# Batch normalization over 64 tiles: each of the two DMA rings is given one transfer at a time

## The chip, the cores and the metric

The kernel runs on one core of a Trainium2 chip. The metric is the device time of one execution in microseconds (us). A TensorE clock of 1.0 is granted in the run, and TensorE does no work here.

## The reference

```python
def reference(x, gamma, beta, running_mean, running_var):   # x: 32 x 256 x 128 x 128 float32
    eps = 1e-5
    ...                                                     # the four vectors, one value per channel
    return gamma * (x - mean) / np.sqrt(var + eps) + beta
```

Every element of x is multiplied by one number of its channel and another number is added. x has 537 MB and so has the result: 1,074 MB pass between HBM and the on-chip memory.

## The kernel before

x is seen as 64 tiles of 128 partitions (128 channels) by 16384 float32, 8.39 MB each; a partition's row is 64 KB and contiguous in HBM. There are three tile buffers, `bufs[0]` to `bufs[2]`, and tile i lives in buffer i mod 3. The work on a tile is a load, one operation in place, and a store:

- SyncE (SP) issues all loads (line 94 for tiles 1 to 63). Its queue is one DMA ring, q1 in the profile. Tile 0 comes in two pieces (lines 84 and 91), with four small loads of the channel vectors between them (line 87).
- VectorE (DVE) scales and shifts the tile in place: `compute`, line 122, one instruction over 16384 columns. For tile 0 there are two, for the last tile VectorE does 9216 columns and ScalarE the other 7168 (line 145).
- ScalarE (ACT) issues all stores: `store`, line 133. Its queue is the other ring, q10.

Both rings are served by the same 16 DMA engines: each transfer is spread over all 16, eight rows of 64 KB to an engine, and each engine adds one to the transfer's semaphore when its own eight rows are through. A transfer has ended when its semaphore has risen by 16.

The order is kept by semaphores written out by hand. `loaded[s]` counts the loads into buffer s, `stored[s]` the stores from it, `done` the operations. A load of tile i waits until the store of tile i - 3 has ended, since both use one buffer; a store waits for its tile's operation. Nothing else holds a load or a store back. So a load can be issued while the load before it is still running, and a store while the store before it is running: the second one then queues on the ring behind the first.

Before the loop, a short chain on VectorE and ScalarE (lines 85 to 117) turns the four vectors into one scale and one shift for each channel; it ends before the first quarter of tile 0 is worked on.

Of the kernel before, what the change touches and what calls it, by code (L numbers as in the profile page):

```python
# [1 line left out]

# [4 lines left out]


NBUF = 3

VCOLS = 9216


@with_exitstack
def kernel(
    ctx: ExitStack,
    tc: tile.TileContext,
    x: bass.AP,
    gamma: bass.AP,
    beta: bass.AP,  # L20
    running_mean: bass.AP,
    running_var: bass.AP,
    out: bass.AP,
):
    nc = tc.nc
    eps = 1e-5
    f32 = mybir.dt.float32

    N, C, H, W = x.shape
    P = nc.NUM_PARTITIONS  # L30
    assert C % P == 0
    NCB = C // P
    HW = H * W
    NT = N * NCB
    B = 32
    NQ = P // B
    NE = 16
    NPAR = 4

    xr = x.rearrange("n (cb p) h w -> (n cb) p (h w)", p=P)  # L40
    outr = out.rearrange("n (cb p) h w -> (n cb) p (h w)", p=P)

    params = ctx.enter_context(tc.tile_pool(name="params", bufs=1))
    data = ctx.enter_context(tc.tile_pool(name="data", bufs=1))
    bufs = [data.tile([P, HW], f32, name=f"t{s}", tag=f"t{s}") for s in range(NBUF)]
    rows = params.tile([B, NPAR * C], f32, name="rows", tag="rows")
    turned = params.tile([B, NPAR * C], f32, name="turned", tag="turned")
    par = params.tile([P, NPAR, NCB], f32, name="par", tag="par")
    eps_t = params.tile([P, 1], f32, name="eps_t", tag="eps")
    std_t = params.tile([P, NCB], f32, name="std_t", tag="std")  # L50
    rstd_t = params.tile([P, NCB], f32, name="rstd_t", tag="rstd")
    scale_t = params.tile([P, NCB], f32, name="scale_t", tag="scale")
    ms_t = params.tile([P, NCB], f32, name="ms_t", tag="ms")
    shift_t = params.tile([P, NCB], f32, name="shift_t", tag="shift")

    loaded = [tc.alloc_semaphore(f"loaded{s}") for s in range(NBUF)]
    stored = [tc.alloc_semaphore(f"stored{s}") for s in range(NBUF)]
    early = tc.alloc_semaphore("early")  # L60
    done = tc.alloc_semaphore("done")
    fetched = tc.alloc_semaphore("fetched")
    vec = tc.alloc_semaphore("vec")
    act = tc.alloc_semaphore("act")

    with tc.tile_critical():  # L66
        count = [0]

        def step(inst, sem=None, value=None):

            if sem is not None:
                inst._wait_ge(sem, value)
            elif count[0]:
                inst._wait_ge(vec, count[0])
            inst.then_inc(vec, 1)
            count[0] += 1
            return count[0]

        left, right = slice(0, HW // 4), slice(HW // 4, HW)
        last = NT - 1  # L80

        nc.sync.dma_start(out=bufs[0][:, left], in_=xr[0][:, left]).then_inc(early, 16)
        zeroed = step(nc.vector.memset(rows[:], 0.0))  # L85
        for r, ap in enumerate((running_var, gamma, beta, running_mean)):
            inst = nc.sync.dma_start(out=rows[0:NE, r * C : (r + 1) * C], in_=ap.partition_broadcast(NE))  # L87
            if r == 0:
                inst._wait_ge(vec, zeroed)
            inst.then_inc(fetched, 16)  # L90
        nc.sync.dma_start(out=bufs[0][:, right], in_=xr[0][:, right]).then_inc(loaded[0], 16)  # L91
        for i in range(1, NT):
            s, turn = i % NBUF, i // NBUF
            inst = nc.sync.dma_start(out=bufs[s][:], in_=xr[i]).then_inc(loaded[s], 16)
            if turn:
                inst._wait_ge(stored[s], 16 * turn)


        step(nc.vector.memset(eps_t[:], eps))  # L99
        step(nc.vector.transpose(out=turned[:], in_=rows[:]), fetched, 16 * NPAR)  # L100

        blocks = turned.rearrange("p (rc q b) -> p rc q b", q=NQ, b=B)
        flat = par.rearrange("p r cb -> p (r cb)")
        for q in range(NQ):
            placed = step(nc.vector.tensor_copy(out=flat[q * B : (q + 1) * B], in_=blocks[:, :, q, 0]))  # L105
        var_t, gamma_t, beta_t, mean_t = (par[:, r] for r in range(NPAR))
        nc.scalar.activation(  # L107
            out=std_t[:],
            in_=var_t,
            func=mybir.ActivationFunctionType.Sqrt,  # L110
            bias=eps_t[:],
            scale=1.0,
        )._wait_ge(vec, placed).then_inc(act, 1)
        step(nc.vector.reciprocal(out=rstd_t[:], in_=std_t[:]), act, 1)  # L114
        step(nc.vector.tensor_mul(out=scale_t[:], in0=gamma_t, in1=rstd_t[:]))  # L115
        step(nc.vector.tensor_mul(out=ms_t[:], in0=mean_t, in1=scale_t[:]))  # L116
        ready = step(nc.vector.tensor_sub(out=shift_t[:], in0=beta_t, in1=ms_t[:]))  # L117
        nc.vector.wait_ge(vec, ready)

        def compute(i, cols=slice(0, HW)):  # L120
            t, cb = bufs[i % NBUF], i % NCB
            return nc.vector.tensor_scalar(  # L122
                out=t[:, cols],
                in0=t[:, cols],
                scalar1=scale_t[:, cb : cb + 1],
                scalar2=shift_t[:, cb : cb + 1],
                op0=mybir.AluOpType.mult,
                op1=mybir.AluOpType.add,
            ).then_inc(done, 1)

        def store(i, after):
            s = i % NBUF
            nc.scalar.dma_start(out=outr[i], in_=bufs[s][:])._wait_ge(done, after).then_inc(stored[s], 16)  # L133

        compute(0, left)._wait_ge(early, 16)
        compute(0, right)._wait_ge(loaded[0], 16)
        store(0, 2)
        for i in range(1, last):
            compute(i)._wait_ge(loaded[i % NBUF], 16 * (i // NBUF + 1))
            store(i, i + 2)  # L140

        turns = last // NBUF + 1
        compute(last, slice(0, VCOLS))._wait_ge(loaded[last % NBUF], 16 * turns)
        t, cb = bufs[last % NBUF], last % NCB
        nc.scalar.activation(  # L145
            out=t[:, VCOLS:],
            in_=t[:, VCOLS:],
            func=mybir.ActivationFunctionType.Identity,
            bias=shift_t[:, cb : cb + 1],
            scale=scale_t[:, cb : cb + 1],  # L150
        )._wait_ge(loaded[last % NBUF], 16 * turns).then_inc(done, 1)
        store(last, last + 3)

        for s in range(NBUF):
            nc.sync.wait_ge(stored[s], 16 * ((NT - s + NBUF - 1) // NBUF))


# [1 line left out]
_INS = ['x', 'gamma', 'beta', 'running_mean', 'running_var']  # L159
_OUTS = [((32, 256, 128, 128), 'float32')]  # L160


# [23 lines left out]
```

## Time and profile before

| what | value |
|---|---|
| median of the runs | 2505.82 us (2505.62 to 2506.52, 3 runs) |
| profiled execution, its own time | 2505.62 us |
| its span | 2503.8 us |
| DMA, mean over the span | 429 GB/s |
| share of the 16 engines' span, loads (q1) and stores (q10) | 49.8% and 49.6% |
| VectorE busy | 564.0 us (23%) |
| a load from issue to landing, median | 58.3 us |
| a store from issue to landing, median | 49.8 us |

The span is what the trace covers; the execution's own time is 1.8 us longer. The first lines of the profile's page say how long each engine was busy; the section on the DMA queues says what share of the time of all 16 DMA engines the packets of each ring took. "Issue to landing" counts from the instruction that starts a transfer to the last increment of its semaphore, so time spent queued on the ring is in it. The trace also holds a record of each DMA packet, with its ring, start, duration and size, and the time of each semaphore increment. A packet of this kernel's large transfers is one row of 64 KB.

### The profile page before, as it was taken

Reading aid. Unit: us, or ns where it says so; the run is one execution under the profiler, and the core shown is the slowest. Engines: PE = TensorE matmul, PEld = TensorE weight load, DVE = VectorE, ACT = ScalarE, POOL = GpSimd, SP = SyncE. Lnnn points to the kernel's source line nnn. Section 1 sums busy time; section 2 is a strip of 40 time slices with the busy share of each in tenths; the row PEclk is TensorE's granted clock in tenths of the full one; section 3 lists DMA queues with packets and bytes.
Section 4 is the critical chain, followed back from the end, with each engine's and each line's share of the span. In section 5 each row is a group of like instructions: output and inputs, shape, how many; then the busy total and the mean of one; then the engine's idle time right before and its main releaser. Section 6 shows DMA issues by size and latency. Waiting matters only on the chain.

```text
span 2503.8 us, 266 instructions
## 1 busy us (share of the span) xinstructions
DVE 564.0 (23%) x76; ACT 7.9 (0%) x3; POOL 0.2 (0%) x4
## 2 busy tenths in 40 slices
DVE  3121221212212122121221212212122122221220
ACT  0000000000000000000000000000000000000001
POOL 0000000000000000000000000000000000000000
DMA  9999999999999999999999999999999999999997
GB/s 419 434 436 431 428 430 433 434 434 433 432 436 432 433 433 427 430 429 433 436 431 429 428 432 433 429 428 436 432 429 428 434 434 429 426 434 435 436 434 316
DMA packets 18706, 1073.83 MB, mean 429 GB/s; under 512 B 2128, under 2 KB 2192, under 8 KB 2192
## 3 DMA queue, kind: packets, MB, share of 16 engines
q1 hardware_dynamic: 9488, 536.94, 49.8%
q10 hardware_dynamic: 9216, 536.88, 49.6%
q14 instruction: 2, 0.02, 0.0%
HBM read 536.94 MB, written 536.87 MB: 429 GB/s over the span
## 4 chain that ended last, share of the span: by engine, by line
another core or an unknown queue 75%; DVE 22%; DMA 2%; ACT 0%; issue 0%; SPq 0%; ACTq 0%; DVEq 0%
DVE t L122 22%; DMA t<-in_x_dram 2%; ACT t L145 0%; SPq L87 0%; DVE rows L85 0%; SPq L91 0%; ACTq L133 0%; DVE eps_t L99 0%; DVEq L181 0%; SPq L66 0%
## 5 line engine op out<-in xcount | busy, mean ns | idle before, releaser
L122 DVE TENSOR_SCALAR t<-t,scale_t,shift_t 128x16384 f32<-128x16384 f32 (+2 forms) x65 | 560.5, 8624 | 1903.6 <-DMA t<-in_x_dram 1903.4
L145 ACT ACTIVATE t<-t,shift_t,scale_t 128x7168 f32<-128x7168 f32 x1 | 6.4, 6361 | 2459.8 <-DMA t<-in_x_dram 2459.8
L100 DVE STREAM_TRANSPOSE turned<-rows 32x1024 f32<-32x1024 f32 x1 | 1.2, 1233 | 7.3 <-DMA rows<-in_running_mean_dram 7.3
L107 ACT ACT_TABLE_LOAD x1 | 1.3, 1283 | 0.9 <-SPq L66 0.9
L85 DVE MEMSET rows<- 32x1024 f32 x1 | 0.9, 912 | 1.2 <-SPq L66 1.2
L105 DVE COPY par<-turned 32x8 f32<-32x8 f32 x4 | 0.6, 162 | 0.1
L107 ACT ACTIVATE std_t<-par,eps_t 128x2 f32<-128x2 f32 x1 | 0.3, 295 | 9.4 <-DVE par L105 9.4
L114 DVE RECIPROCAL rstd_t<-std_t 128x2 f32<-128x2 f32 x1 | 0.2, 166 | 0.4 <-ACT std_t L107 0.4
L117 DVE TENSOR_TENSOR shift_t<-par,ms_t 128x2 f32<-128x2 f32 x1 | 0.2, 163 | 0.0
L116 DVE TENSOR_TENSOR ms_t<-par,scale_t 128x2 f32<-128x2 f32 x1 | 0.2, 161 | 0.0
L115 DVE TENSOR_TENSOR scale_t<-par,rstd_t 128x2 f32<-128x2 f32 x1 | 0.2, 161 | 0.0
L170 POOL MEMSET const-bfloat16-1.0<- 128x1 bf16 x1 | 0.1, 102 | 0.0
L170 POOL MEMSET const-uint8-127<- 128x1 uint8 x1 | 0.1, 102 | 0.0
L170 POOL MEMSET const-float32-0.0<- 128x1 f32 x1 | 0.1, 99 | 0.2 <-issue 0.2
L170 POOL MEMSET const-float32-1.0<- 128x1 f32 x1 | 0.1, 99 | 0.0
L99 DVE MEMSET eps_t<- 128x1 f32 x1 | 0.1, 59 | 0.1
## 6 DMA issues: line engine op xcount, KB each, us to landing
t<-in_x_dram SPq DMA_DIRECT2D x1, 6144.0 KB, 19.6
t<-in_x_dram SPq DMA_DIRECT2D x1, 2048.0 KB, 7.7
out_dram<-t ACTq DMA_DIRECT2D x64, 49.8
t<-in_x_dram SPq DMA_DIRECT2D x63, 58.3
rows<-in_running_var_dram SPq DMA_DIRECT2D x1, 16.0 KB, 6.4
rows<-in_gamma_dram SPq DMA_DIRECT2D x1, 16.0 KB, 6.2
rows<-in_beta_dram SPq DMA_DIRECT2D x1, 16.0 KB, 6.0
rows<-in_running_mean_dram SPq DMA_DIRECT2D x1, 16.0 KB, 6.1
```

Source lines behind the costliest of these rows:

```text
L85: zeroed = step(nc.vector.memset(rows[:], 0.0))
L99: step(nc.vector.memset(eps_t[:], eps))
L100: step(nc.vector.transpose(out=turned[:], in_=rows[:]), fetched, 16 * NPAR)
L105: placed = step(nc.vector.tensor_copy(out=flat[q * B : (q + 1) * B], in_=blocks[:, :, q, 0]))
L107: nc.scalar.activation(out=std_t[:], in_=var_t, func=mybir.ActivationFunctionType.Sqrt, bias=eps_t[:], scale=1.0,)._wait_ge(vec, placed).t ...
L114: step(nc.vector.reciprocal(out=rstd_t[:], in_=std_t[:]), act, 1)
L115: step(nc.vector.tensor_mul(out=scale_t[:], in0=gamma_t, in1=rstd_t[:]))
L116: step(nc.vector.tensor_mul(out=ms_t[:], in0=mean_t, in1=scale_t[:]))
L117: ready = step(nc.vector.tensor_sub(out=shift_t[:], in0=beta_t, in1=ms_t[:]))
L122: return nc.vector.tensor_scalar(out=t[:, cols], in0=t[:, cols], scalar1=scale_t[:, cb : cb + 1], scalar2=shift_t[:, cb : cb + 1], op0=myb ...
L145: nc.scalar.activation(out=t[:, VCOLS:], in_=t[:, VCOLS:], func=mybir.ActivationFunctionType.Identity, bias=shift_t[:, cb : cb + 1], scale ...
L170: nc = _bacc.Bacc("TRN2", target_bir_lowering=False, num_devices=1)
```

## The change

A load of tile i (for i from 2) now waits for the end of the load of tile i - 1 as well as for its buffer: the wait for the buffer becomes an instruction of its own on SyncE ahead of the load, and the load itself carries the wait for its predecessor. A store of tile i (for i from 1 to 62) is preceded on ScalarE by a wait for the end of the store of tile i - 1. The store of the last tile gets no such wait, and neither does the load of tile 1. Sizes, buffers, operations and the order of the instructions on each engine stay as they are; the line numbers after the first edit shift by 4.

```diff
         for i in range(1, NT):
             s, turn = i % NBUF, i // NBUF
+            if turn:
+                nc.sync.wait_ge(stored[s], 16 * turn)
             inst = nc.sync.dma_start(out=bufs[s][:], in_=xr[i]).then_inc(loaded[s], 16)
-            if turn:
-                inst._wait_ge(stored[s], 16 * turn)
+            if i >= 2:
+                inst._wait_ge(loaded[(i - 1) % NBUF], 16 * ((i - 1) // NBUF + 1))
...
         def store(i, after):
             s = i % NBUF
-            nc.scalar.dma_start(out=outr[i], in_=bufs[s][:])._wait_ge(done, after).then_inc(stored[s], 16)
+            inst = nc.scalar.dma_start(out=outr[i], in_=bufs[s][:]).then_inc(stored[s], 16)
+            inst._wait_ge(done, after)
+
+        def turn_of_store(i):
+            nc.scalar.wait_ge(stored[(i - 1) % NBUF], 16 * ((i - 1) // NBUF + 1))
...
         for i in range(1, last):
             compute(i)._wait_ge(loaded[i % NBUF], 16 * (i // NBUF + 1))
+            turn_of_store(i)
             store(i, i + 2)
```

## The prediction

> **What bounds the kernel now.** I read the page's first lines, then the DMA queues.
>
> ```profile
> span 2503.8 us, 266 instructions
> DVE 564.0 (23%) x76; ACT 7.9 (0%) x3; POOL 0.2 (0%) x4
> DMA  9999999999999999999999999999999999999997
> ...
> q1 hardware_dynamic: 9488, 536.94, 49.8%
> q10 hardware_dynamic: 9216, 536.88, 49.6%
> ```
>
> The two rings fill 99.4% of the time of the 16 DMA engines; no compute engine is near its limit. Then who waits for whom, of the engines and of SP's queue, and the issues with their time to landing:
>
> ```profile
> DVE t L122 <- DMA t<-in_x_dram: 1903.4, 64, 31.4
> ...
> SPq L94 <- DMA out_dram<-t: 2391.3, 61, 67.6
> ...
> out_dram<-t ACTq DMA_DIRECT2D x64, 49.8
> t<-in_x_dram SPq DMA_DIRECT2D x63, 58.3
> ```
>
> VectorE waits for loads and loads wait for buffers. 58.3 + 8.8 + 49.8 = 116.9 us is one turn of a buffer, three tiles, so a tile takes 39.0 us. Both transfers last longer than that: part of each is queueing behind its predecessor, and that queue is what the change removes.
>
> The period shows in the timeline, as the distance from one 128x16384 operation to the next (first column):
>
> ```profile
> 53.05 8.81 DVE L122 TENSOR_SCALAR t<-t,scale_t,shift_t 128x16384 f32<-128x16384 f32 x1 [22.79 <-DMA t<-in_x_dram]
> 93.26 8.81 DVE L122 TENSOR_SCALAR t<-t,scale_t,shift_t 128x16384 f32<-128x16384 f32 x1 [31.40 <-DMA t<-in_x_dram]
> ...
> 248.63 8.81 DVE L122 TENSOR_SCALAR t<-t,scale_t,shift_t 128x16384 f32<-128x16384 f32 x1 [29.88 <-DMA t<-in_x_dram]
> ...
> 406.19 8.81 DVE L122 TENSOR_SCALAR t<-t,scale_t,shift_t 128x16384 f32<-128x16384 f32 x1 [30.91 <-DMA t<-in_x_dram]
> 446.36 8.81 DVE L122 TENSOR_SCALAR t<-t,scale_t,shift_t 128x16384 f32<-128x16384 f32 x1 [31.36 <-DMA t<-in_x_dram]
> ...
> 2201.07 8.81 DVE L122 TENSOR_SCALAR t<-t,scale_t,shift_t 128x16384 f32<-128x16384 f32 x1 [29.86 <-DMA t<-in_x_dram]
> ...
> 2433.07 8.81 DVE L122 TENSOR_SCALAR t<-t,scale_t,shift_t 128x16384 f32<-128x16384 f32 x1 [29.83 <-DMA t<-in_x_dram]
> 2471.74 5.08 DVE L122 TENSOR_SCALAR t<-t,scale_t,shift_t 128x9216 f32<-128x9216 f32 x1 [29.85 <-DMA t<-in_x_dram]
> ```
>
> It is (2471.74 - 53.05) / 62 = 39.01 us on average, 38.84 in the four tiles from 93.26, 40.17 at its worst, and 38.67 in the six from 2201.07.
>
> The packet records say why. Per tile an engine moves 16 packets of 64 KB. The usual one takes 2.418 us, back to back, whether the rings alternate (from 35 us on) or one runs alone (loads at 23 to 32 us, the last store). That is 38.65 to 38.69 us per tile, the floor. The rest, 0.36 us per tile, is stretched packets (up to 1.5 us longer) on the engines furthest behind: following the records end to start, stretch comes to 12 us on the mean engine and about 22 us on the worst, over the run. The worst engines do not idle; the others wait for them. The 16 increments of a load's semaphore spread over 0.7 us at tile 1, 5 us around tile 9, 26 us from tile 32 to the end. So in the second half 11 or 12 engines have an empty ring whenever a load or store is issued: they already run with one transfer per ring. The other 4 or 5 never do. The change puts all 16 into that state and stops the drift.
>
> **The change, part by part.**
>
> *The gap in a ring.* Rows of the records: a contested ring gives its increment after the other ring's next packet, 2.4 + 0.3 us; the slowest engine adds at least 0.7 (tile 1's spread); SP issues 0.02 us after a landing (112.38 to 112.40); the first packet follows 0.9 us after issue on idle engines (last store), 2.6 us where engines are busy (the store at 1627). Sum 4.4 to 6.1 us, rounded up to whole packets: three, 7.3 us. In it the other ring runs alone at the same 2.418 us per packet, so the engine loses nothing while the two gaps do not meet. The fast engines of the second half show this: with gaps of about four packets in each ring, they follow at 38.67 us per tile. Cost: 0, covered by the other ring's transfer; if that cover is gone, see the third rival.
>
> The rule that speaks against the change is in the Trainium skill, "DMA: Bandwidth & Descriptors", section "Anatomy of one DMA — SWDGE (gpsimd) path": about 2.0 us fixed per transfer, mostly the receipt of the last byte. It is told for the other issue path; taken for all 124 transfers that now wait and laid bare, it would be an estimated 248 us more. The trace sides against laying it bare: a lone ring's packets fill the engine.
>
> *Do the gaps meet?* Count from the start. Load 1's last packets end at 49.5 to 50.3 us; store 0 began at 35.0, alternating, and has some five of its eight packets left. Load 1 lands at 53.0, load 2 starts at about 57; store 0 runs three packets alone, two alternating, ends at about 62 and lands near 65. Store 1 is issued then, 12 us after load 1 landed and 3 us after its operation ended (61.86). Each ring's gap now lies in the middle of the other's transfer, two packets or more off either end, and since both gaps are about the same length the lag should stay.
>
> *Starting a transfer on an empty ring.* This is what each load and store does now. The first store did so at 30.3 us with all engines in step: it stretched the packets in flight by 0.05 to 0.70 us, 0.46 on the mean. Over all stores that met an empty ring, the mean is 0.13 us per engine; for loads 0.01. So 0.14 us per tile, at most 0.46 + 0.01.
>
> *The stretch per tile afterwards.* What counts is the stretch of the engine that ends last. From below: the mean engine's whole-run stretch, 12/64 = 0.19 us. From above: the worst engine of each tile, added up as if every tile waited for it anew, 53.6 us over 63 tiles = 0.85. Between them: from 875 to 2125 us, where most engines start transfers on empty rings, the mean engine has 0.26 us per tile; the run's ratio of worst to mean, 22/12, makes that 0.47. I take 0.47, since rings with a gap still let an engine lag by a packet or two. Period 38.65 + 0.47 = 39.12, against 39.01: 62 x 0.11 = +7 us. Ends: 0.19 gives 62 x (38.84 - 39.01) = -10.5 us; 0.85 gives 62 x 0.49 = +30 us.
>
> *Queues and waits.* 61 wait instructions on SP and 62 on ACT lie inside the gaps. Behind SP's stands only the next load. Behind ACT's wait stand its store and, at the end, ScalarE's part of the last tile (L145): store 62 should be issued some 20 us before that tile lands, so it is in time; failing that, it costs up to its 6.4 us. The buffer wait is met long before the load's turn. Load 2, queued at 4.87 us before, is issued at 53.0; store 0 covers that.
>
> *The end.* Store 63 has no wait for its predecessor and joins the ring behind store 62, which has some packets left to cover the last operation (6.36 us), as now. Fast engines finish some 14 us early now and would not; that helps nobody. 0, at most 3 us.
>
> **Sum.** 2505.6 + 7 + 0 = 2512.6 us for the execution; the profiled run stands 0.2 us below the median, so 2512.6.
>
> **Rivals.**
> 1. *Staying in step is itself cheaper*: engines are stretched because they are out of step, so all tiles go like the early ones (38.84). For it: the stretch grew with the spread, to 39.3 and 40.17 at 3 to 8 us of it. Against: with the largest spread the period was lowest, 38.67. 2505.6 - 10.5 = 2495 us.
> 2. *Nothing changes*: the same engines carry the same stretch, 2505.6 us. For it: most engines already run so. Against: starts on empty rings become universal.
> 3. *Gaps meet*: stores are slower to restart than loads, the lag grows until load i and store i - 2 both wait for store i - 3. Both rings are then empty for 0.33 + 0.67 + 0.02 + 0.95 = 2.0 us per tile: 62 x 2.0 = +122 us, 2628. It decides once the lag grows from 12 to nearly a whole period of 39 us. Against: the fast engines show no such drift.
>
> **How the numbers follow.** A measurement of this kernel can tell about 0.2% (5 us) from no change. Forecast (2512.6, own range 2505 to 2532): 0.50, of which 0.10 ends within 5 us. Rival 1: 0.33, of which 0.30 is faster and 0.03 within. Rival 2: 0.10. Rival 3: 0.07. Faster 0.30, same 0.23, slower 0.47. The range 2492 to 2545 takes in the -10.5 end with a few us of scatter and the +30 end with the end's 3 and L145's 6; it leaves out rival 3 and tails of some 0.1.
>
> **What would show it.** Right: landings of a load spread under 5 us throughout; each ring with three or four packets' gap; DMA share still 99%; load issue to landing about 36 us and store about 34; a period near 39.1 without a late stretch at 38.67; SP waiting for loads, not stores. Rival 1: the period stays at 38.8. Rival 3: SP waits for stores, DMA share near 95%, period near 41. The prediction is wrong if an engine alone on one ring does not keep 2.418 us per packet, or if most starts cost the first store's 0.46 us (62 x 0.33 = +20 us on top).

## The result and the profile after

The changed kernel takes 2487.69 us (median of 4, 2485.97 to 2489.02) beside 2505.72 us, a ratio of 0.9928 with a 95% interval of 0.9911 to 0.9946: 0.7% faster, where I had said 0.3% slower. Its profiled execution takes 2486.43 us with a span of 2484.7. The page of the changed kernel:

```profile
span 2484.7 us, 389 instructions
DVE 564.0 (23%) x76; ACT 7.9 (0%) x3; POOL 0.2 (0%) x4
DMA  9999999999999999999999999999999999999999
...
q1 hardware_dynamic: 9488, 536.94, 50.1%
q10 hardware_dynamic: 9216, 536.88, 49.9%
```

The rings now fill the whole span, 100.0% against 99.4%. Then SP's queue waits and the issues:

```profile
SPq L98 <- DMA t<-in_x_dram: 1378.8, 62, 48.0
SPq L97 <- DMA out_dram<-t: 1009.0, 61, 16.8
...
out_dram<-t ACTq DMA_DIRECT2D x64, 38.6
t<-in_x_dram SPq DMA_DIRECT2D x63, 38.6
```

From load 2 to store 62 nothing queues on a ring any more: both transfers last one period. SP waits first for the buffer (line 97, the store of tile i - 3, at most 16.8 us) and then for the preceding load (line 98). The timeline:

```profile
52.87 8.81 DVE L126 TENSOR_SCALAR t<-t,scale_t,shift_t 128x16384 f32<-128x16384 f32 x1 [22.86 <-DMA t<-in_x_dram]
...
247.22 8.81 DVE L126 TENSOR_SCALAR t<-t,scale_t,shift_t 128x16384 f32<-128x16384 f32 x1 [29.91 <-DMA t<-in_x_dram]
...
401.81 8.81 DVE L126 TENSOR_SCALAR t<-t,scale_t,shift_t 128x16384 f32<-128x16384 f32 x1 [29.84 <-DMA t<-in_x_dram]
418.74 0.34 ACTq L137 DMA_DIRECT2D out_dram<-t  x1
440.43 8.81 DVE L126 TENSOR_SCALAR t<-t,scale_t,shift_t 128x16384 f32<-128x16384 f32 x1 [29.81 <-DMA t<-in_x_dram]
...
2415.80 8.81 DVE L126 TENSOR_SCALAR t<-t,scale_t,shift_t 128x16384 f32<-128x16384 f32 x1 [29.82 <-DMA t<-in_x_dram]
2454.43 5.08 DVE L126 TENSOR_SCALAR t<-t,scale_t,shift_t 128x9216 f32<-128x9216 f32 x1 [29.82 <-DMA t<-in_x_dram]
```

The period is (2454.43 - 52.87) / 62 = 38.74 us, against 39.01 before and 38.65 at the floor. That is 17.1 of the 19.1 us of span; tile 1 comes 0.2 us earlier and the stretch from the last tile's operation to the end is 1.8 us shorter (30.3 against 32.1). In the packet records the stretched time over the floor's 2.418 us per packet falls from 12.1 to 5.3 us per engine, and from about 22 to 7 us on the worst engine. (The records do not name the engine; a packet is put on the engine whose last packet ends where it starts.) A store is issued 16.9 us after its load has landed (401.80 to 418.74), and this *distance* is the same in nearly every tile; the next load is issued at the landing itself. The distance is what most of the experiments are about.

### The profile page after: what moved, and what is told of

It reads as the page before. It is cut to its first block, busy times and chain, and to the rows that moved or that the text cites. A ratio compares the mean times of both kernels' runs of the same rounds, so it can differ in the third digit from the quotient of the medians.

```text
span 2484.7 us, 389 instructions
## 1 busy us (share of the span) xinstructions
DVE 564.0 (23%) x76; ACT 7.9 (0%) x3; POOL 0.2 (0%) x4
## 3 DMA queue, kind: packets, MB, share of 16 engines
q1 hardware_dynamic: 9488, 536.94, 50.1%
## 4 chain that ended last, share of the span: by engine, by line
DMA 99%; ACT 0%; SPq 0%; issue 0%; DVE 0%; DVEq 0%
DMA t<-in_x_dram 99%; ACT t L154 0%; SPq L87 0%; DVE rows L85 0%; SPq L91 0%; DVE eps_t L103 0%; DVEq L190 0%; SPq L66 0%
## 6 DMA issues: line engine op xcount, KB each, us to landing
out_dram<-t ACTq DMA_DIRECT2D x64, 38.6
t<-in_x_dram SPq DMA_DIRECT2D x63, 38.6
```

## The experiments

In the table, "stretch" is the stretched packet time per engine over the whole run, from the packet records. "Starts apart" is the shortest time between the issue of a load and of a store, as it repeats from tile to tile, with the one that is issued first; where transfers queue (before, every second and every eighth tile, the two kernels without turns) the packets can start later than the issue. The rows under the changed kernel are in the order of the text.

| kernel | median us (runs) | ratio to before, 95% | period us | stretch us | starts apart, us |
|---|---|---|---|---|---|
| before | 2505.72 (4) | 1 | 39.01 | 12.1 | 10.3 to 14.1, store |
| changed | 2487.69 (4) | 0.9928 (0.9911 to 0.9946) | 38.74 | 5.3 | 16.9, load |
| loads only | 2510.81 (10) | 1.0011 (0.9999 to 1.0023) | 39.05 | 22.8 | 8.9, load |
| stores only | 3236.94 (4) | 1.2909 (1.2888 to 1.2931) | 50.79 | 394 | 0.06, load |
| every second tile | 2493.39 (4) | 0.9946 (0.9931 to 0.996) | 38.87 | 13.9 | 8.0 and 21.7 in turn, store |
| every eighth tile | 2523.74 (4) | 1.0068 (1.005 to 1.0085) | 39.20 | 27.0 | 0.06 at each turn, load |
| late store, no turns | 2519.26 (10) | 1.0034 (1.0005 to 1.0063) | 39.14 | 24.7 | 3.0 to 5.8, store |
| uneven start, no turns | 2511.00 (10) | 1.0018 (1.0008 to 1.0027) | 38.78 from tile 2 | 13.4 | 15.3 to 15.9, store |
| turns, distance 12.1 | 2489.89 (4) | 0.9936 (0.9921 to 0.9951) | 38.84 | 9.7 | 12.1, load |
| turns, distance 21.8 | 2485.20 (4) | 0.9918 (0.9903 to 0.9933) | 38.68 | 4.7 | 16.9, store |
| turns, distance 26.6 | 2483.99 (4) | 0.9915 (0.9898 to 0.9931) | 38.59 | 1.3 | 12.0, store |
| turns, distance 31.5 | 2485.21 (12) | 0.9931 (0.9911 to 0.9951) | 38.58 | 3.8 | 7.2, store |
| turns, distance about 38 | 2588.12 (4) | 1.0333 (1.0312 to 1.0354) | 40.14 | 93.7 | 2.3 to 2.8, store |
| stores only, pause of two | 2728.59 (2) | 1.0892 (1.0869 to 1.0915) | 42.45 | 110 | 1.9, load |

(A pause before store 1 shortens the first periods of its run, which is why two periods stand below the floor; from tile 2 on they are 38.66 and 38.70.)

**Loads alone.** The edit, on the changed kernel:

```diff
-            turn_of_store(i)
             store(i, i + 2)
```

> Only the loads take turns; stores are issued as before the change. Three theories for the 17 to 19 us that the whole change saved (period 39.01 to 38.74 us per tile). A, out of step: packets get stretched on engines that have fallen a packet or more behind the others, and the change bounds how far they fall behind. B, queued successor: a second transfer queued behind the first on a ring stretches packets where the two meet; the spread of the engines is a by-product. C, position: what helps is that a store now starts about 17 us after its load has landed and not 9 us. A: a load's landings stay within 5 us, so nearly the whole gain, 2487 to 2492 us. B: 131 of the 194 us of stretched packet time before lay on loads, so about two thirds of the gain at most, 2493 to 2497 us. C: the stores are where they were, 2504 to 2507 us.

Measured 2510.81 us: nothing of the gain. Yet the 16 increments of a load lie within 5 us of each other, as in the changed kernel. The issues of this run, and one load and store of its timeline:

```profile
out_dram<-t ACTq DMA_DIRECT2D x64, 39.8
t<-in_x_dram SPq DMA_DIRECT2D x63, 41.0
...
603.69 0.33 SPq L98 DMA_DIRECT2D t<-in_x_dram  x1
...
612.54 0.34 ACTq L137 DMA_DIRECT2D out_dram<-t  x1
```

So hardly anything queues, and the engines are in step: A and B both fall short as they stand. The stretch is larger than before the change (22.8 us per engine), nearly all on loads, and the records show where: on the load packet in flight just ahead of a store's first packet, about 0.2 us on each engine, store after store. C comes nearest, though the median lies 4 us above its range; the store is issued 8.9 us after the load in every tile.

**Stores alone.**

```diff
             inst = nc.sync.dma_start(out=bufs[s][:], in_=xr[i]).then_inc(loaded[s], 16)
-            if i >= 2:
+            if False:
                 inst._wait_ge(loaded[(i - 1) % NBUF], 16 * ((i - 1) // NBUF + 1))
```

> Only the stores take turns; loads are issued as soon as their buffer is free, as before the change. A (out of step): engines are held together once per tile by the stores, 2487 to 2492 us. B (queued successor): the third of the stretch that lay on stores is saved, 2498 to 2502 us. C (position of the store): nearly everything, 2486 to 2490 us.

Measured 3236.94 us, 29% slower; no theory had that. The timeline of this run, one period:

```profile
995.19 8.81 DVE L126 TENSOR_SCALAR t<-t,scale_t,shift_t 128x16384 f32<-128x16384 f32 x1 [41.97 <-DMA t<-in_x_dram]
1046.16 8.81 DVE L126 TENSOR_SCALAR t<-t,scale_t,shift_t 128x16384 f32<-128x16384 f32 x1 [42.16 <-DMA t<-in_x_dram]
1046.32 0.33 SPq L98 DMA_DIRECT2D t<-in_x_dram  x1
1046.38 0.34 ACTq L137 DMA_DIRECT2D out_dram<-t  x1
```

The load of tile i waits for its buffer, the store of tile i - 3; the store of tile i - 2 waits for its turn, which is the same store. SP and ACT issue 0.06 us apart, in all periods but one. This is my third rival. It costs far more than its 2.0 us per tile: about 6 us without a packet and 6 us of stretch per engine and tile, on packets all through the transfers.

**Every second and every eighth tile** (the same edit with 8 for 2):

```diff
-            if i >= 2:
+            if i >= 2 and i % 2 == 0:
...
-            turn_of_store(i)
+            if i % 2 == 0:
+                turn_of_store(i)
```

> Loads and stores take turns at every second tile only; at the others the next transfer may queue behind its predecessor, if its buffer is free. A (out of step): two tiles are too short to fall far behind (2.6 us of spread at tile 4 before the change), so 2487 to 2493 us. B (queued successor): half of the queued seams are back, about half of the gain, 2495 to 2499 us. C: position changes only on every second tile, about 2496 us.

> Turns on both rings at every eighth tile only. Theory A: within eight tiles an engine falls 4 us behind (tiles 1 to 9 before the change) and is caught up again; the period stays near 38.8 to 39.2 and a quarter to a half of the gain is left, 2494 to 2502 us. Theory B (queued successor): seven of eight seams are queued, 2503 to 2506 us.

Measured 2493.39 us for every second tile, just above the upper end of A and half of the gain or more; 2523.74 us for every eighth, slower than before, which no theory allowed. The tiles around its turn at tile 16, from the timeline of the run with every eighth:

```profile
603.83 8.81 DVE L126 TENSOR_SCALAR t<-t,scale_t,shift_t 128x16384 f32<-128x16384 f32 x1 [30.76 <-DMA t<-in_x_dram]
648.56 8.81 DVE L126 TENSOR_SCALAR t<-t,scale_t,shift_t 128x16384 f32<-128x16384 f32 x1 [35.91 <-DMA t<-in_x_dram]
661.56 0.33 SPq L98 DMA_DIRECT2D t<-in_x_dram  x1
661.62 0.34 ACTq L137 DMA_DIRECT2D out_dram<-t  x1
683.92 8.81 DVE L126 TENSOR_SCALAR t<-t,scale_t,shift_t 128x16384 f32<-128x16384 f32 x1 [26.55 <-DMA t<-in_x_dram]
723.15 8.81 DVE L126 TENSOR_SCALAR t<-t,scale_t,shift_t 128x16384 f32<-128x16384 f32 x1 [30.42 <-DMA t<-in_x_dram]
```

Three periods of 44.73, 35.36 and 39.23 us make 119.3, 3.4 over the floor, and the records have 124 us of stretched packets (all engines together) in them. Each of the seven turns of a store ends with the store issued 0.06 us after a load, the common start of the run before, once in eight tiles. Nor do the turns bring the engines back in step: the increments of a load lie 9 to 19 us apart from tile 11 on. So this run does not test theory A; how its loss divides between the common starts and the tiles between them was not worked out.

**A late store without turns.** The edit, on the kernel before (the spare tile's two lines and the activation's semaphore left out):

```diff
+            if 0 < i < last:
+                nc.scalar.wait_ge(done, after)
+                for j in range(5):
+                    nc.scalar.activation(out=idle_t[:], in_=idle_t[:], ...)   # 128x1800, 1.8 us each
             nc.scalar.dma_start(out=outr[i], in_=bufs[s][:])._wait_ge(done, after).then_inc(stored[s], 16)
```

> The kernel before, without any turn, but ScalarE spends about 8 us on five small operations on a spare tile between the end of a tile's operation and its store (tiles 1 to 62), so that a store is issued some 17 us after the load has landed, as with the change. A (out of step) and B (queued successor): no help, the engines drift apart as before, 2503 to 2510 us. C (position): 2486 to 2490 us and landings in step.

The store is issued 16.2 us after the landing, and the run takes 2519.26 us, from 2492 to 2543: C falls, and the time lies above A and B too.

```profile
1010.52 0.34 ACTq L148 DMA_DIRECT2D out_dram<-t  x1
1014.13 0.33 SPq L95 DMA_DIRECT2D t<-in_x_dram  x1
```

The next load is now issued 3.0 to 5.8 us after the store. A store's distance from its own load's landing is not enough while loads start when they like. The stretch moves to the stores' first packets (14.7 of 24.7 us per engine). The engines drift 19 us apart in their loads.

**An uneven start without turns.** The edit, on the kernel before (the new semaphore's line left out):

```diff
         nc.sync.dma_start(out=bufs[0][:, right], in_=xr[0][:, right]).then_inc(loaded[0], 16)
+        for j in range(5):
+            nc.sync.dma_start(out=bufs[2][2 * j : 2 * j + 2], in_=xr[2][2 * j : 2 * j + 2]).then_inc(uneven, 16)
         for i in range(1, NT):
             s, turn = i % NBUF, i // NBUF
+            if i == 2:
+                nc.sync.wait_ge(uneven, 16 * 5)
```

> The kernel before, with five loads of two rows each (two rows of 64 KB, meant for two of the 16 DMA engines, one row each) put on the load ring between tile 0 and tile 1; load 2, which overwrites their rows, waits for them. It makes two engines 12 us late from the start. The two have 12 us more to move, so 2505 + 12 = 2517 us if they also get the 22 us of stretch that the worst engine had. Theory A (an engine is stretched because it is behind): the period is 39.2 us or more from the first tiles on and the end is at 2515 to 2525 us. Theory E (particular engines are slow, whether behind or not): the two late ones are the mean kind, 12 us of stretch and 12 us late, and the end is at 2504 to 2509 us.

Load 1's increments came at 52.4 to 52.9 us from 14 engines and at 83.5 and 84.6 from two: the two were late as meant, and by more than 12 us, since store 0 took turns with the extra rows and their packets were stretched by some 10 us. The run took 2511.00 us, between the two forecasts, but the period decides. Three operations of this run:

```profile
305.86 8.81 DVE L127 TENSOR_SCALAR t<-t,scale_t,shift_t 128x16384 f32<-128x16384 f32 x1 [29.81 <-DMA t<-in_x_dram]
344.51 8.81 DVE L127 TENSOR_SCALAR t<-t,scale_t,shift_t 128x16384 f32<-128x16384 f32 x1 [29.84 <-DMA t<-in_x_dram]
383.14 8.81 DVE L127 TENSOR_SCALAR t<-t,scale_t,shift_t 128x16384 f32<-128x16384 f32 x1 [29.82 <-DMA t<-in_x_dram]
```

The engines are 26.5 us apart here, and the period is the floor, 38.63 to 38.65; the kernel before had 39.3 to 40.2 at this place with 3 to 8 us. From tile 2 to the end it is 38.78. Between 100 and 345 us the two late engines have 2.2 and 1.6 us of stretch, the other fourteen 3.1 to 4.7. So an engine is not stretched for being behind. Theory A is refuted by this run; the first 84 us and the extra rows cost what the period gives back.

**The distance.** With turns on both rings, one pause early in the run should move all stores for good. The edit, on the changed kernel (2, 4, 5 or 7 operations; for the shorter distance the pause stands ahead of load 2 instead; the spare tile and the function `pause` left out):

```diff
             turn_of_store(i)
+            if i == 1:
+                pause(4)             # four operations on a spare tile, 1.8 us each
             store(i, i + 2)
```

> The changed kernel, and ScalarE spends about 3.6 us on two small operations on a spare tile once, before store 1. With turns on both rings a store is issued a fixed time after its load has landed (16.9 us with the change); this one pause should move it to about 20 us for the whole run. Theory A (out of step): the engines are held in step as before, so 2486 to 2490 us. Theory D (position): what stretches packets is where in a load a store begins, so the time moves with the position, by some 5 us or more one way or the other. Theory C (a store soon after its operation is bad): no change, 2486 to 2490 us.

> As the run before, with a pause of about 7.3 us before store 1: a store is issued about 24 us after its load has landed. A and C: 2486 to 2490 us. D: another time than with 17 and 20 us.

> The changed kernel, and load 2 waits about 3.6 us longer, once, after load 1 has landed: a store is issued about 9 to 13 us after its load has landed for the whole run, as in the kernel with turns for loads alone, but with turns on both rings. A: 2487 to 2492 us, since the engines are in step. C and D: stretched load packets at the start of each store come back, 2500 to 2515 us.

> The changed kernel with one pause of about 13 us before store 1; stores are then issued some 31 us after their load has landed, 8 us short of a whole period. Stretch fell with this distance so far (12.1, 16.9, 21.8 and 26.6 us: 2489.9, 2487.7, 2485.2 and 2484.0 us). If only the distance to the operation's end matters, 2483 to 2485 us again; if the two rings' gaps begin to touch here, idle time appears and the run takes 2490 us or more.

It did, in steps of two packets (4.8 us). 2489.89, 2487.69, 2485.20 and 2483.99 us at 12.1, 16.9, 21.8 and 26.6 us: a flat stretch with a slight slope, all well under the kernel before. From tile 2 on the periods of these four runs are 38.73, 38.74, 38.72 and 38.66 us. No step is the 5 us that D asked for, and the last two times lie below the 2486 that A and C gave as the least. One period at 26.6 us:

```profile
1015.58 0.33 SPq L99 DMA_DIRECT2D t<-in_x_dram  x1
...
1042.15 0.34 ACTq L139 DMA_DIRECT2D out_dram<-t  x1
```

C's and D's 2500 to 2515 us at the short distance were wrong: of its stretch some 60 of 155 us, summed over the engines, lie in the first 250 us, before the distance settles. The longest pause went past the flat part. SP's queue waits and one period of that run:

```profile
SPq L98 <- DMA out_dram<-t: 2268.4, 61, 39.0
SPq L99 <- DMA t<-in_x_dram: 205.8, 62, 48.7
...
1048.86 0.34 ACTq L139 DMA_DIRECT2D out_dram<-t  x1
1051.25 0.33 SPq L99 DMA_DIRECT2D t<-in_x_dram  x1
```

The store has slid to 2.4 us ahead of a load's issue, and the run takes 2588.12 us with its landings within 3 us of each other: engines in step, one transfer per ring, and 3.3% slower than before. Without a packet an engine is some 11 us in all; 94 us per engine are stretch. I had expected idle time to be the price.

To see whether the slope is real and where the flat part ends, three kernels ran on one chip:

> The changed kernel once more, beside the next two on the same chip: 2486 to 2489 us, a store issued 16.9 us after its load has landed.

> The changed kernel with the pause of 7.3 us before store 1 again (store issued 26.6 us after its load has landed). Theory D (position of the starts): 2483 to 2485 us, 3 us or more under the changed kernel on the same chip. If the earlier difference was one between chips, equal to it within 1 us.

> The same with a pause of five operations, about 9 us; the distance moved in steps of two packets (4.8 us) so far, so it should be 31.5 us, between the best (26.6) and the bad (37.5, 2588 us). Theory D with a gap of about 7 us in each ring: the store's gap would end where the load's begins, still without touching, 2483 to 2490 us. If it falls to the next step, 37 us, 2580 to 2590 us.

2486.32 us (2484.59 to 2489.03) for the changed kernel, 2484.90 (2483.68 to 2487.16) at 26.6 us and 2485.21 (2484.01 to 2487.47) at 31.5, 12 runs each. The later store is 1.4 us ahead of the change by the medians, with ranges that overlap: too little to call it better, and neither forecast (3 us or more, within 1 us) was met. The stretch at 26.6 us is 4.6 us per engine here, where the first run had 1.3, beside 5.5 for the changed kernel: the small differences within the flat part do not repeat. The flat part reaches to a store issued 7.2 us ahead of the next load. Of 29 runs of the kernel before beside them, 27 took 2498 to 2510 us and two took 2483.34 and 2484.48: the old kernel can fall into a good arrangement by itself, though no trace of such a run was taken.

**What a common start costs, and two causes tried.** On the kernel with turns for stores alone (the line for `flat_out` left out):

```diff
-            inst = nc.scalar.dma_start(out=outr[i], in_=bufs[s][:]).then_inc(stored[s], 16)
+            at = P * i + (4 if i < last - 1 else 0)
+            inst = nc.scalar.dma_start(out=flat_out[at : at + P], in_=bufs[s][:]).then_inc(stored[s], 16)
```

> Turns for stores alone (3237 us: load and store start at the same moment in each period), with the rows of tiles 0 to 61 written four rows (256 KB) further on in the output; the output is displaced by that, and its first four rows are not written. Theory D1: packets are stretched because an engine's load and store packets of equal row number, whose HBM addresses differ by a multiple of 8 MB, run at once; the displacement takes that relation away and the stretch (some 6.6 us per engine and tile) mostly goes: 2800 to 2950 us. Theory D2: the moment of starting is what matters, whatever the addresses: 3200 to 3270 us.

3227.96 us: moving the output by 256 KB changes nothing. With a pause of two operations, and then one, ahead of each store from store 4 on:

> Turns for stores alone (3237 us), with about 3.6 us of small operations on ScalarE ahead of each store from store 4 on, so that a load starts one to two packets before the store that is released at the same moment. Theory F (the stretch of 6.3 us per engine and tile there comes from load and store moving the same row, that is the same partition, side by side): it mostly goes while the empty time grows by up to 3.6 us, 2950 to 3100 us. If the common start is what costs whatever the row: no less than 3237 us, up to 3460.

> Turns for stores alone (3237 us) with one small operation, about 1.9 us, ahead of each store from store 4 on. A load then starts about 2 us before the store released with it, less than a packet, so an engine still moves equal rows of load and store one after the other. Theory F (equal rows side by side): the stretch stays, 3150 to 3350 us. Theory D (starting at one moment): it goes as with two operations, 2650 to 2800 us.

Two operations make the run 508 us *faster*, 2728.59 us. A period of that run:

```profile
1031.23 43.02 SPq L99 DMA_DIRECT2D t<-in_x_dram  x2
1031.29 3.62 ACT L147 ACTIVATE idle_t<-idle_t,eps_t 128x1800 f32<-128x1800 f32 x2 [39.37 <-DMA out_dram<-t]
1033.13 0.34 ACTq L139 DMA_DIRECT2D out_dram<-t  x1
```

The store is issued 1.9 us after the load, and the stretch falls from 394 to 110 us per engine; both forecasts had more time. One operation changed nothing (3232.44 us), for a plain reason: ACT issued the store 0.09 us after SP's load, while the operation ahead of it was still running, so the starts were not parted at all. That run is inconclusive. Whether the rows or the start mattered was left to a last one, with the store in two halves (the waits on `stored`, which count to 32 for a store here, left out):

```diff
-            inst = nc.scalar.dma_start(out=outr[i], in_=bufs[s][:]).then_inc(stored[s], 16)
+            inst = nc.scalar.dma_start(out=outr[i][P // 2 :], in_=bufs[s][P // 2 :]).then_inc(stored[s], 16)
             inst._wait_ge(done, after)
+            nc.scalar.dma_start(out=outr[i][: P // 2], in_=bufs[s][: P // 2]).then_inc(stored[s], 16)
```

> Turns for stores alone (3237 us), each store issued as two transfers of 64 partitions, the upper half first, so that an engine's store rows are no longer its load rows at the same moment, while load and store still start together. Theory F (equal rows side by side on one engine): the stretch of 6.3 us per engine and tile mostly goes, 2700 to 2950 us. Theory D (a common start): it stays, 3150 to 3350 us.

3256.97 us: other rows, the same cost. The stretch is even larger, 573 us per engine, and has moved to the stores (353 us, where the run with whole stores has 86). Theory F falls; of what was tried, only parting the starts (0.06 to 1.9 us) lowers the cost.

## Why the prediction was wrong, step by step

The direction was wrong, and the time lies under the range's lower end of 2492 us.

- *The bound and the floor*: right. The engines' packets set the time, at 38.65 us per tile.
- *The gap in a ring*: right. Load 1's last packets end at 49.5 to 50.1 us, load 2's first start at 56.7 to 59.5, so a gap is three or four packets. It costs nothing: the rings fill 100.0% of the span. The 2.0 us per transfer of the rule that I weighed do not show in the time: the period is 0.09 us over the floor.
- *Where the gaps lie*: right in kind. I counted 12 us from a landing to the next store's issue and an even lag afterwards; it is 16.9, and even. That miscount did not decide the time: the run with 12.1 us takes 2489.89 us. Landings spread over 3.5 to 4.8 us in nearly every tile from tile 5 on, under the 5 I gave.
- *Starting on an empty ring*: mis-sized. I took 0.13 us per store and 0.01 per load from the kernel before. In the changed kernel the same window after each issue has 0.034 and 0.005, first store included. A load's own first row mostly lies behind that window; its stretch adds 0.03 per load.
- *The stretch per tile afterwards*: the step that failed. I took 0.47 us on the path, between 0.19 and 0.85; the period is 38.74 - 38.65 = 0.09 us over the floor. All three values carried the old kernel's stretch into a kernel in which loads and stores start at other moments. Of the 5.3 us per engine that are left, 4.7 lie on the first rows of loads and on load packets beside a store's first row. The runs show in its place that, where transfers do not queue, stretch follows when a store starts between two loads. Per engine and tile (the table's stretch over 64) it is 6.2 us with the store 0.06 us behind the load, 1.7 at 1.9, 0.36 with loads alone at 8.9, 0.15 at 12.1 and 0.08 at 16.9; counted back from the next load it is 0.07 at 16.9 us ahead, 0.02 to 0.07 at 12.0, 0.06 at 7.2 and 1.5 at 2.4. Which one is first matters: 8.9 us behind a load costs six times what 7.2 us ahead of one does, though the run at 8.9 also differs in that its stores take no turns. The change fixes the store's place for the whole run where it costs little.
- *The end*: 1.8 us gained where I had 0 and at most 3 lost.
- *Issue to landing*: 38.6 us for both, where I wrote 36 and 34. The next issue follows a landing within 0.1 us, so the whole period lies between issue and landing; I had subtracted the gap, which is inside it.
- *SP's waits*: half right, the wait for the store comes first in the order of SP's instructions and takes 1009 us.
- *Rival 1* (in step is cheaper) gave 2495 us and the right sign, for a reason that did not hold: in step and slow (loads alone; distance 38), out of step by 26.5 us and at the floor (the uneven start).
- *Rival 3* (gaps meet) is no part of this change, but half of the change alone produces it. Its price was wrong: (50.79 - 39.01) = 11.8 us per tile, not 2.0.

Two slips in the sums move nothing: the worst period of the old timeline is 40.21 us, the first, not 40.17, and 2505.8 + 7 for the median is 2512.8, not 2512.6.

That the kernel before loses its 22 us for the same cause, its engines drifting one by one through bad distances, fits the stretched packets at the first rows of transfers (8.5 of its 12.1 us per engine), and the two fast runs of it. It is argued, not shown: no run held the drift and changed the distances alone. The issues alone do not explain it: for stores 1 to 61 of that kernel the store is issued 10.3 to 14.1 us ahead of the next load, and with turns 12.0 us ahead costs 0.02 to 0.07 us per engine and tile, here 0.19. What differs is that transfers queue there, so on the engines behind they start at other moments than they are issued; which of these moments cost the time stays open. What inside the engines or the memory makes two starts disturb each other was not found; a shift of 256 KB in HBM and another order of the rows did not lower the cost of the common start.

## What to carry to other kernels

Where two rings keep the DMA engines full, look at when the transfers of one start against those of the other: with turns on both rings, a store issued 12 us or more after a load and 7 us or more ahead of the next ran near the floor here, in a period of 39 us, and a common start cost 29%. A fixed distance is not enough by itself: with turns for loads alone the store came 8.9 us after the load in every tile, and nothing was gained. Waiting for the predecessor on both rings fixes the distance and cost nothing here while the other ring's transfer covered the gap; doing it on one ring alone, or only now and then, can lock both to one event. And a loss read off the old trace as "so much per packet" may belong to the old timing, so a change of timing needs a wider bound, below as well as above.

## What was not expected of the hardware

- Load and store transfers of 8.39 MB issued 0.06 us apart every period: 50.79 us per pair; with turns on both rings and 16.9 us apart, 38.74 us.
- The usual packet of 64 KB takes 2.418 us on an engine whether one ring or both are busy and in either direction; an engine's increment for a finished transfer comes only after one packet of the other ring, 2.7 us after the last row's end on a contested ring (the medians of the changed kernel) and 0.3 us on an idle one (the last store).
- A DMA behind one small operation on ScalarE is issued without waiting for that operation's end (0.09 us after SP's issue, the operation taking 1.8).
